# Plain 128-row blocks for x and the result, and a 128-row low-part pass of the scores, in a one-core transformer layer

## The chip, the cores and the metric

The kernel runs on one core of one Trainium2 chip. The metric is the device time of one execution in microseconds (us). Three runs of the kernel before gave 637.65, 639.62 and 641.45 us; the median is 639.62 us. One further execution was taken with the hardware profiler.

## The reference

One layer over 256 tokens of width 1024, in float32:

```python
cs = jax.nn.silu(c)
mod = cs @ ada_w[l] + ada_b[l]
sh1, sc1, g1, sh2, sc2, g2 = jnp.split(mod[:, None, :], 6, axis=-1)
h = rms_norm(x, norm1_g[l]) * (1.0 + sc1) + sh1
x = x + g1 * token_mixer(h, ...)
h = rms_norm(x, norm2_g[l]) * (1.0 + sc2) + sh2
x = x + g2 * hier_moe(h, ...)
return rms_norm(x, final_g)
```

`token_mixer` projects h with one wide matrix and runs two branches: a diagonal complex state-space scan with a gated output, and grouped attention (16 heads of 64, 4 key groups) with compressed, selected and window keys. `hier_moe` sends each token to 2 of 32 experts (1024 to 256 to 1024).

## The kernel before

**Order of tokens.** On the chip a block of 128 tokens does not lie in its natural order: row 32 j + c of block b holds token 128 b + 4 c + j, which is what the scan over chunks of four tokens wants. The order is made by the load of x (line 109): its source is a view "(c j) d -> j c d", four groups of 32 rows, each row 4 KB. The results leave through the inverse view (lines 1347 and 1355), as four transfers of 128 rows by 512 columns, 2 KB a row. Line 1355 issues each as soon as its part is scaled by line 1354 (VectorE) or lines 1351 and 1352 (ScalarE, then GpSimd).

**Start.** SyncE issues all plain loads in one in-order queue: x block 0, a small pack of constants (line 111), x block 1, then in turn the eight 1 MB slices of the modulation weights (`ada1`, line 121) and eight 512 KB slabs of the first projections (line 128), with further constants between. VectorE makes masks and index tiles (lines 143 to 185); GpSimd makes the identity, some iotas, and sets large tiles to zero: `Vc` (128 x 5120, line 489), `B0` (128 x 1024, line 491), `bw` (128 x 4096, line 493) and `Tt` (line 571). Per block of x, ScalarE sums squares (line 213), VectorE takes the reciprocal root (`rsqrt1`, lines 192 to 197) and scales (line 215), and TensorE transposes (line 219). Then a loop over eight slices (lines 357 to 374) makes the modulation vectors and the first four projections, while VectorE also prepares the scan.

**Three-pass matmuls.** Most products are done in float32r as three passes of a high and a low part (`mm3`, lines 270 to 273): high x high, high x low, low x high.

**Attention.** Each of the 16 heads has three score tiles s0, s1, s2, each made by `score` (line 881): a pass of 128 rows whose lower and upper 64 rows hold the high and the low part of q against the high part of the keys (`KS`, written twice, line 882), a pass of 64 rows for the high part of q against the low part of the keys (`KL`, line 883), then one or two bf16 matmuls that add masks (line 885). 48 score tiles in all. VectorE takes maxima (lines 891 to 893), ScalarE exponentials (line 900), GpSimd scales (line 905), TensorE transposes (lines 910 and 912) and multiplies by the values (line 922). Projections and gates are put between the heads as filler. `KL` has two key groups side by side on its upper and lower 64 rows.

**After attention.** Output projections (lines 970 to 1033), then line 1041 puts the residual x into four accumulators `acc` by a matmul with the identity, in the order in which x lies. The experts (lines 1274 to 1300) gather tokens with 0/1 matrices, stream 96 MB of weights through rings of buffers (lines 1284 to 1291), and add their results to `acc` with 0/1 matrices built from token numbers `tok1` (lines 182 to 185). Two sums of squares and `rsqrt1` end the kernel.

**What sets the order.** The framework lays out the instructions of each engine at build time, by the order of the program and a simulated time line of its own, and adds the waits. Each engine then runs its list in that order.

Of the kernel before, what the change touches and what calls it, by code (L numbers as in the profile page):

```python
# [9 lines left out]
F32 = mybir.dt.float32  # L10
F32R = mybir.dt.float32r
BF16 = mybir.dt.bfloat16
AF = mybir.ActivationFunctionType
ALU = mybir.AluOpType
# [39 lines left out]
def hybrid(ctx: ExitStack, tc: tile.TileContext, A, out, dbg=None, stop=None):  # L54
    nc = tc.nc
# [5 lines left out]
    def f32(ap):  # L61
        return ap.bitcast(F32)
# [44 lines left out]
    x = cp.tile([128, 2, D], F32, name="x")  # L107
    for b in range(2):
        nc.sync.dma_start(x[:, b], A["x"][0, 128 * b:128 * b + 128].rearrange("(c j) d -> j c d", j=4))
        if b == 0:  # L110
            nc.sync.dma_start(pk[:, 0:NPK0], A["pk"][:, 0:NPK0])
# [25 lines left out]

    ident = cp.tile([128, 128], F32, name="ident")
    G.memset(ident, 1.0)  # L140
# [40 lines left out]
    V.tensor_scalar(desc, itok1[:, 0:8], -1.0, 9.0, op0=ALU.mult, op1=ALU.add)  # L181
    iq1 = pp.tile([128, 2, 2], I32, name="iq1")
    G.iota(iq1, pattern=[[128, 2], [0, 2]], base=1, channel_multiplier=1)
    tok1 = cp.tile([128, 2, 2], F32, name="tok1")
    V.tensor_copy(tok1, iq1)

# [198 lines left out]
    Tt = sp.tile([128, 16, 128], F32, name="Tt")  # L385
    Vc = sp.tile([128, 16, 2, 160], F32, name="Vc")
    Vt = Vc[:, :, :, 32:160]
# [100 lines left out]

    G.memset(Vc, 0.0)
    B0 = pp.tile([128, 16, 2, 32], F32, name="B0")  # L490
    G.memset(B0, 0.0)
    bw = pp.tile([128, 16, 2, 128], F32, name="bw")
    G.memset(bw, 0.0)
    bcur = [[pp.tile([128, 16, 16], F32, name=f"b{r}{i}") for r in range(2)] for i in range(2)]
# [178 lines left out]
    KS = at.tile([128, 4, 528], F32R, name="KS")  # L673
    KL = at.tile([128, 2, 528], F32R, name="KL")

    def keys(nm, offs):
        o = proj_T(nm)
        for gp in range(2):
            own = slice(64 * gp, 64 * gp + 64)
            for b in range(2):  # L680
                src = o[own, :, 128 * b:128 * b + 128]
                for hv in range(2):
                    hs = slice(64 * hv, 64 * hv + 64)
                    dst = KS[hs].rearrange("p (m two) t -> p m two t", two=2)[:, :, gp, offs[b]:offs[b] + 128]
                    (S.copy if hv == gp else V.tensor_copy)(dst, src)
                V.tensor_sub(KL[own, :, offs[b]:offs[b] + 128], src,
                             f32(KS[own].rearrange("p (m two) t -> p m two t", two=2)[:, :, gp, offs[b]:offs[b] + 128]))
# [33 lines left out]
    for g in range(4):  # L721
        gs = slice(64 * (g % 2), 64 * (g % 2) + 64)
        S.copy(KS[:, g, 256:272], pkc[:, 16 * g:16 * g + 16])
        V.tensor_sub(KL[gs, g // 2, 256:272], pkc[gs, 16 * g:16 * g + 16], f32(KS[gs, g, 256:272]))
    vcn = at.tile([64, 64], F32, name="vcn")
# [130 lines left out]
    for qc in range(4):  # L856
# [13 lines left out]
        for ii in range(2):  # L870
            for gp in range(2):
# [3 lines left out]
                nm = f"{qc}{ii}{gp}"  # L875
                q_hi = QS[own, ii, gp]
                s0 = psb.tile([128, 512], F32, name=f"s0{nm}", tag="s", bufs=3)
# [3 lines left out]
                def score(s_, t0, c0, n, masks):  # L881
                    T.matmul(s_[:, 0:n], lhsT=QS[:, ii, gp, t0:t0 + 128], rhs=KS[:, g, c0:c0 + n], start=True, stop=False)
                    T.matmul(s_[:, 0:n], lhsT=q_hi[:, t0:t0 + 128], rhs=KL[own, G2_, c0:c0 + n], start=False, stop=False)  # L883
                    for z, (a_, b_, m_) in enumerate(masks):
                        T.matmul(s_[:, a_:b_], lhsT=identb, rhs=m_, start=False, stop=z == len(masks) - 1)
# [73 lines left out]
    mgs = ctx.enter_context(ExitStack())  # L959
    mg = mgs.enter_context(tc.tile_pool(name="mg", bufs=1))  # L960
    G2, sh2 = Gm[:, 1], modT[:, 2]
    g1b, g2b = gb
# [75 lines left out]
    with tc.issue_after(pe_last[0].ins):  # L1038
        for h in range(2):
            for b in range(2):  # L1040
                T.matmul(acc[b][h], lhsT=ident, rhs=x[:, b, 512 * h:512 * h + 512], start=True, stop=False)
    dbg("x2", x)
# [302 lines left out]
    for b in range(2):  # L1345
        rsqrt1(rstd3[:, b:b + 1], ss3[:, b, 1:2], part3[:, b:b + 1], mo, f"r3{b}")
    ov = out[0].rearrange("(b c j) d -> b j c d", b=2, j=4)
    for b, c0, n in ((0, 0, 512), (0, 512, 512), (1, 0, 512), (1, 512, 512)):
        c, a_ = slice(c0, c0 + n), acc[b][c0 // 512][:, c0 % 512:c0 % 512 + n]
        if (b, c0) == (1, 0):  # L1350
            S.activation(x[:, b, c], a_, AF.Copy, scale=rstd3[:, b:b + 1])  # L1351
            G.tensor_mul(x[:, b, c], x[:, b, c], fg[:, c])  # L1352
        else:
            V.scalar_tensor_tensor(x[:, b, c], a_, rstd3[:, b:b + 1], fg[:, c], op0=ALU.mult, op1=ALU.mult)  # L1354
        nc.sync.dma_start(ov[b][:, :, c], x[:, b, c])
    return

def _lay(i):
# [50 lines left out]
    o["adat"] = np.stack([a.transpose(1, 0, 2) for a in two + one])  # L1410
    for n in ("x", "ada_b"):
        o[n] = i[n]
    o["fg"] = i["final_g"][None]
# [21 lines left out]
```

## Time and profile before

| what | us |
|---|---|
| median of three runs | 639.62 |
| the profiled execution's own time | 639.31 |
| span of the profile, first to last instruction | 637.6 |
| busy in the span: TensorE matmul (PE) / weight load (PEld) | 521.3 / 357.3 |
| busy in the span: VectorE (DVE) / ScalarE (ACT) / GpSimd (POOL) | 358.9 / 205.3 / 219.2 |
| moved by DMA | 168.11 MB |

A busy share is a mean over stages with different limits; the rows further down are therefore taken stage by stage. A matmul's duration in the profile contains its way through the pipeline, so the pace of TensorE is read from the distance of the starts of two matmuls. "PEclk" is the granted TensorE clock (1.00 is 2.4 GHz, 0.50 is 1.2 GHz). "DMA share" is the mean busy share of the core's 16 DMA engines.

### The profile page before, as it was taken

The numbers are of one execution on the slowest core, as the hardware profiler recorded it, in microseconds if no ns is written. First come the engines' busy times: TensorE is split into PE (matmuls) and PEld (weight loads), VectorE is DVE, ScalarE is ACT, GpSimd is POOL, SyncE is SP. The second block draws the span as 40 slices with busy tenths as digits, with TensorE's granted clock in tenths as the row PEclk, the third lists the DMA queues.
The fourth block names the chain that finished last, engine by engine and source line by source line (L and its number), as shares of the span: only waits on it lengthen the run. The fifth ranks groups of instructions, "written<-read, shape, count | busy, mean of one in ns | idle before, by whom it ended". The sixth has DMA issues, their size and how long they took to land. (4 is left out here: it accounts for less than half of the span.)

```text
span 637.6 us, 10548 instructions
## 1 busy us (share of the span) xinstructions
PE 521.3 (82%) x4027; PEld 357.3 (56%) x4028; DVE 358.9 (56%) x940; ACT 205.3 (32%) x469; POOL 219.2 (34%) x316
## 2 busy tenths in 40 slices
PE   0367799688887999999999996999988887867760
PEld 0255588477886878788888994443442242312120
DVE  9699965999476766567776767433330222302041
ACT  1365336433244554354543453112120111101030
POOL 7058405567478432696987005000000000000000
PEclk9997899797998999999999999799997999979795
DMA  8885355766545332653379797199999999999941
GB/s 175 283 325 176 114 186 187 275 228 256 196 155 182 117 100 67 222 198 142 94 269 346 284 421 291 62 371 398 423 418 423 419 420 422 420 421 420 408 167 67
DMA packets 27795, 168.11 MB, mean 264 GB/s; under 512 B 3034, under 2 KB 3162, under 8 KB 10202
## 3 DMA queue, kind: packets, MB, share of 16 engines
q1 hardware_dynamic: 25434, 158.97, 65.5%
q0 software_dynamic: 2304, 8.39, 3.9%
q8 instruction: 34, 0.56, 0.4%
q14 instruction: 23, 0.19, 0.1%
HBM read 166.30 MB, written 1.05 MB: 262 GB/s over the span
## 5 line engine op out<-in xcount | busy, mean ns | idle before, releaser
L1191 PE MATMUL guq<-gu,x 128*32 128x512 f32 (+1 forms) x512 | 101.0, 673 | 27.0 <-DMA gu<-in_egu_dram 26.3
L1352 POOL TENSOR_TENSOR x<-x,fg 128x512 f32<-128x512 f32 x1 | 1.3, 1267 | 222.3 <-ACT x L1351 222.3
L1191 PEld LDWEIGHTS guq<-gu,x 128*32 128x32 f32 (+1 forms) x512 | 22.9, 124 | 85.5 <-DMA gu<-in_egu_dram 46.4
L905 POOL TENSOR_SCALAR pr<-pr,st 128x128 f32<-128x128 f32 (+1 forms) x64 | 35.9, 577 | 35.2 <-DVE st L902 29.2
L336 POOL TENSOR_SCALAR adt<-adt,ct 128x256 f32<-128x256 f32 x64 | 39.6, 633 | 22.5 <-DMA adt<-in_adat_dram 22.3
L1212 PE MATMUL dnq<-ed,acq 128*32 128x512 f32 (+1 forms) x224 | 39.0, 598 | 2.8 <-ACT acq L1206 1.9
L1200 DVE SCALAR_TENSOR_TENSOR pk<-pk,guq 128x256 f32<-128x256 f32 x9 | 3.8, 420 | 62.5 <-ACT pk L1199 62.5
L1216 DVE SCALAR_TENSOR_TENSOR gb<-dnq,wsq,gb 128x512 f32<-128x512 f32 (+1 forms) x20 | 13.8, 696 | 40.5 <-PE dnq L1212 40.5
L1162 DVE TENSOR_SCALAR x<-pgq,Gm,modT 128x256 f32<-128x256 f32 (+1 forms) x20 | 10.3, 516 | 43.4 <-PE pgq L1156 23.4
L900 ACT ACTIVATE pr<-s,st 128x128 f32<-128x128 f32 (+1 forms) x64 | 26.1, 420 | 24.0 <-DVE st L896 22.8
L1160 ACT ACTIVATE x<-pgq,modT,Gm 128x256 f32<-128x256 f32 (+1 forms) x20 | 10.8, 541 | 56.0 <-DVE x L1162 25.9
L1217 ACT CAST room<-gb 128x512 fp32r<-128x512 f32 (+1 forms) x20 | 11.4, 575 | 53.5 <-DVE gb L1216 53.5
L1156 PE MATMUL pgq<-room,hTh 128*128 128x256 f32 (+1 forms) x80 | 22.9, 316 | 3.1 <-DVE wsq L1179 1.2
L1199 ACT ACTIVATE pk<-guq 128x256 f32<-128x256 f32 x9 | 3.5, 385 | 66.6 <-PE guq L1191 66.6
L1156 PEld LDWEIGHTS pgq<-room,hTh 128*128 128x128 f32 x80 | 16.1, 202 | 15.6 <-issue 5.7
L1212 PEld LDWEIGHTS dnq<-ed,acq 128*32 128x32 f32 (+1 forms) x224 | 10.7, 113 | 23.4 <-issue 17.6
L219 PE MATMUL ph<-ident,scr 128*128 128x128 f32 x16 | 3.1, 358 | 24.7 <-DVE rstd L197 24.7
L337 POOL TENSOR_TENSOR adt<-adt 128x512 f32<-128x512 f32 x16 | 23.0, 1447 | 0.5
L230 PE MATMUL pm<-ada,csb 128*32 128x256 f32 x256 | 19.7, 415 | 3.8 <-DVE mr L240 3.8
L1156 PE MATMUL pgq<-room,hTl 128*128 128x256 f32 (+1 forms) x80 | 21.1, 294 | 0.0
L883 PE MATMUL s<-KL,QS 64*128 64x272 f32 (+1 forms) x48 | 18.7, 390 | 0.0
L1072 POOL TENSOR_SCALAR gb<-x,rstd 128x256 f32<-128x256 f32 x8 | 4.0, 515 | 39.4 <-ACT xT L1008 39.3
(718 smaller groups left out, 1729.9 us busy)
## 6 DMA issues: line engine op xcount, KB each, us to landing
gu<-in_egu_dram SPq DMA_DIRECT2D x64, 1024.0 KB, 19.8
ed<-in_edn_dram SPq DMA_DIRECT2D x28, 1024.0 KB, 18.0
ada<-in_adat_dram SPq DMA_DIRECT2D x16, 1024.0 KB, 8.8
adt<-in_adat_dram POOLq DMA_DIRECT2D x16, 512.0 KB, 6.1
slab<-in_w_dram SPq DMA_DIRECT2D x8, 512.0 KB, 3.8
cw<-in_cw_dram SPq DMA_DIRECT2D x4, 1024.0 KB, 4.9
win_q<-in_win_dram SPq DMA_DIRECT2D x4, 1024.0 KB, 4.9
win_gs<-in_win_dram SPq DMA_DIRECT2D x4, 1024.0 KB, 7.4
```

The costliest lines, as they stand in the source:

```text
L230: T.matmul(pm_k[32 * t:32 * t + 32, 0:256], lhsT=csb[:, 2 * t + j], rhs=slot[:, 2 * t + j], start=j == 0, stop=j == 1, tile_position=(0, 3 ...
L336: G.tensor_scalar(w[:, t], w[:, t], ct[:, 4 * h + t:4 * h + t + 1], 1.0, op0=ALU.mult, op1=ALU.mult)
L337: G.tensor_add(w[:, 0:2], w[:, 0:2], w[:, 2:4])
L883: T.matmul(s_[:, 0:n], lhsT=q_hi[:, t0:t0 + 128], rhs=KL[own, G2_, c0:c0 + n], start=False, stop=False)
L900: S.activation(pr[:, a_:b_], src, AF.Exp, bias=st[:, 1, z:z + 1], scale=0.125, accum_out=st[:, 2, z:z + 1])
L905: G.tensor_scalar(pr[:, a_:b_], pr[:, a_:b_], st[:, 3, z:z + 1], 1.0, op0=ALU.mult, op1=ALU.mult)
L1156: T.matmul(pg[:, ki, 0:S_], lhsT=h[:, b, 128 * k:128 * k + 128], rhs=O[:, b], start=b + i == 0, stop=b + i == 2)
L1160: S.activation(xk[:, ki, 0:S_], pg[:, ki, 0:S_], AF.Identity, bias=sh2[:, k:k + 1], scale=G2[:, k:k + 1])
L1191: gl_ = T.matmul(gu[r], lhsT=xe[k][:, r], rhs=wgu(e, k), start=k == 0, stop=k == 7, tile_position=(0, s_ * e))
L1212: T.matmul(dn[r], lhsT=ac[:, c, r], rhs=wdn(e, c)[:, 512 * h:512 * h + 512], start=c == 0, stop=c == 1, tile_position=(0, s_ * e))
L1216: V.scalar_tensor_tensor(ty[0:M, c], dn[0:M, c], ws[0:M, 0:1], g2b[0:M, 512 * h + c.start:512 * h + c.stop], op0=ALU.mult, op1=ALU.mult)
L1217: act_last[0] = S.copy(yh[0:M, h, c], ty[0:M, c])
```

## The change

- x is laid out on the host in the order in which the chip wants it; each block is loaded as plain 128 rows.
- A 0/1 matrix `perm` (one VectorE instruction) takes the place of the identity in the four matmuls that put x into `acc`, so that `acc` is in natural order; `tok1` gets permuted token numbers to match; the result leaves as plain 128 rows.
- `KL` becomes 128 rows for each of the four key groups, with zeros in the half that does not belong to the group (two new GpSimd memsets); the low-part pass takes the same 128-row weights as the pass before it.
- The zeroing of `Vc` and `bw` moves from GpSimd to VectorE and to the head of the program; an iota of GpSimd and a cast of VectorE become two small VectorE instructions.

```diff
-        nc.sync.dma_start(x[:, b], A["x"][0, 128 * b:128 * b + 128].rearrange("(c j) d -> j c d", j=4))
+        nc.sync.dma_start(x[:, b], A["x"][b])
...
+    Vc = sp.tile([128, 16, 2, 160], F32, name="Vc")
+    V.memset(Vc, 0.0)
+    bw = pp.tile([128, 16, 2, 128], F32, name="bw")
+    V.memset(bw, 0.0)
     ident = cp.tile([128, 128], F32, name="ident")
...
-    iq1 = pp.tile([128, 2, 2], I32, name="iq1")
-    G.iota(iq1, pattern=[[128, 2], [0, 2]], base=1, channel_multiplier=1)
     tok1 = cp.tile([128, 2, 2], F32, name="tok1")
-    V.tensor_copy(tok1, iq1)
+    for b in range(2):
+        V.tensor_scalar(tok1[:, b], tq.to_broadcast([128, 2]), 128.0 * b + 1.0, None, op0=ALU.add)
...
-    G.memset(Vc, 0.0)
...
-    G.memset(bw, 0.0)
...
-    KL = at.tile([128, 2, 528], F32R, name="KL")
+    KL = at.tile([128, 4, 528], F32R, name="KL")
+    for gp in range(2):
+        G.memset(f32(KL[64 - 64 * gp:128 - 64 * gp].rearrange("p (m two) t -> p m two t", two=2)[:, :, gp]), 0.0)
...
-        V.tensor_sub(KL[gs, g // 2, 256:272], pkc[gs, 16 * g:16 * g + 16], f32(KS[gs, g, 256:272]))
+        V.tensor_sub(KL[gs, g, 256:272], pkc[gs, 16 * g:16 * g + 16], f32(KS[gs, g, 256:272]))
...
                     T.matmul(s_[:, 0:n], lhsT=QS[:, ii, gp, t0:t0 + 128], rhs=KS[:, g, c0:c0 + n], start=True, stop=False)
-                    T.matmul(s_[:, 0:n], lhsT=q_hi[:, t0:t0 + 128], rhs=KL[own, G2_, c0:c0 + n], start=False, stop=False)
+                    T.matmul(s_[:, 0:n], lhsT=QS[:, ii, gp, t0:t0 + 128], rhs=KL[:, g, c0:c0 + n], start=False, stop=False)
...
+    perm = mg.tile([128, 128], F32, name="perm")
+    V.tensor_scalar(perm, itok1[:, 0:128], tq, 1.0, op0=ALU.subtract, op1=ALU.is_equal)
...
-                T.matmul(acc[b][h], lhsT=ident, rhs=x[:, b, 512 * h:512 * h + 512], start=True, stop=False)
+                T.matmul(acc[b][h], lhsT=perm, rhs=x[:, b, 512 * h:512 * h + 512], start=True, stop=False)
...
-    ov = out[0].rearrange("(b c j) d -> b j c d", b=2, j=4)
+    ov = out[0].rearrange("(b p) d -> b p d", b=2)
...
-        nc.sync.dma_start(ov[b][:, :, c], x[:, b, c])
+        nc.sync.dma_start(ov[b][:, c], x[:, b, c])
...
-    for n in ("x", "ada_b"):
-        o[n] = i[n]
+    o["x"] = i["x"][0].reshape(2, 32, 4, 1024).transpose(0, 2, 1, 3).reshape(2, 128, 1024)
+    o["ada_b"] = i["ada_b"]
```

## Rows read from the trace of the kernel before

**Rows 1.** Busy time of each engine in stretches of the span (from the span's start), with the number of instructions; then the granted TensorE clock, the DMA share and GB/s.
```profile
24.00:87.00 63.00, 47.34 (x388) 36.19 (x389) 59.12 (x219) 29.86 (x59) 29.82 (x38) 0.89 0.60 221
200.00:320.00 120.00, 119.52 (x903) 99.97 (x902) 82.19 (x195) 59.78 (x170) 74.37 (x116) 0.99 0.38 131
...
400.00:410.00 10.00, 9.26 (x36) 5.08 (x38) 2.71 (x20) 1.50 (x4) 0.00 (x0) 0.62 0.01 2
...
413.00:613.00 200.00, 167.94 (x970) 64.84 (x972) 46.51 (x112) 25.41 (x51) 0.00 (x0) 0.95 1.01 411
```

**Rows 2.** Waits: who waited for whom, us in total, times, longest. The first is the longest of VectorE from 24 to 87 us, the second the only one of TensorE's matmuls from 200 to 320 us.
```profile
DVE mr L240 <- PE pm L238: 1.2, 2, 1.0
...
PE pj_ga L273 <- DVE ga2l L264: 0.5, 1, 0.5
```

**Rows 3.** The time line from 0 to 30 us: start, duration, engine, line and operation; in brackets the engine's idle time before it and what ended it.
```profile
1.08 0.17 DVE L319 MEMSET onesc<- 128x128 f32 x1
...
1.40 0.22 DVE L149 CAST tk<-itok 128x128 f32<-128x128 int32 x1
1.41 0.06 DVE L1132 MEMSET own<- 64x2 f32 x1
...
2.09 0.59 SPq L109 DMA_DIRECT2D x<-in_x_dram  x1
...
2.14 4.35 POOL L489 MEMSET Vc<- 128x5120 f32 x1
2.21 10.55 DVE L143 CAST identb<-ident 128x128 bf16<-128x128 f32 x1
...
10.88 1.79 POOL L571 MEMSET Tt<- 128x2048 f32 x1
...
21.84 1.06 ACT L213 ACTIVATE scr<-x 128x1024 f32<-128x1024 f32 x1 [5.68 <-DMA x<-in_x_dram]
...
23.02 0.15 DVE L192 TENSOR_SCALAR r11v<-ss 128x1 f32<-128x1 f32 x1 [5.94 <-ACT scr L213]
...
24.69 1.94 PE L219 MATMUL ph<-ident,scr 128*128 128x128 f32 x8 [24.69 <-DVE rstd L197]
```

**Rows 4.** Two stretches of 1 us at the start, columns as in Rows 1: while the second block of x is on its way, and just after it has landed.
```profile
18.00:19.00 1.00, 0.00 (x0) 0.00 (x0) 0.00 (x0) 0.00 (x0) 0.00 (x0) 1.00 1.01 217
...
22.00:23.00 1.00, 0.00 (x0) 0.00 (x0) 0.00 (x0) 0.99 (x2) 0.00 (x0) 1.00 1.01 406
```

**Rows 5.** The two passes of the scores by their lines: min/median/max ns of one, first and last start, shapes.
```profile
L882 PE MATMUL s<-KS,QS x48: 275/288/428, 180.7 to 320.1; 128*128 128x272 f32 x32, 128*128 128x256 f32 x16
...
L883 PE MATMUL s<-KL,QS x48: 379/387/490, 181.0 to 320.4; 64*128 64x272 f32 x32, 64*128 64x256 f32 x16
```

**Rows 6.** The time line of TensorE (columns as in Rows 3) at two score tiles: around 209 us, and at a bf16 mask matmul behind a float32 transposition at 249 us.
```profile
209.21 0.28 PE L271 MATMUL pj_q<-hTh,q1h 128*128 128x256 f32 x1
209.21 0.19 PEld L882 LDWEIGHTS s<-KS,QS 128*128 128x128 f32 x1
...
209.33 0.28 PE L882 MATMUL s<-KS,QS 128*128 128x272 f32 x1
209.54 0.18 PEld L883 LDWEIGHTS s<-KL,QS 64*128 64x128 f32 x1
209.54 0.39 PE L883 MATMUL s<-KL,QS 64*128 64x272 f32 x1
...
209.87 0.29 PE L885 MATMUL s<-mask,identb 128*128 128x272 bf16 x1
...
249.80 0.33 PE L910 MATMUL pta<-ident,pr 128*128 128x128 f32 x1
...
249.97 0.22 PE L885 MATMUL s<-mask,identb 128*128 128x128 bf16 x1
```

**Rows 7.** The time line (columns as in Rows 3) of GpSimd's scaling and of the transpositions that follow it, in two heads.
```profile
239.32 1.62 POOL L905 TENSOR_SCALAR pr<-pr,st 128x128 f32<-128x128 f32 x4 [4.81 <-DVE st L902]
...
243.66 0.24 PEld L910 LDWEIGHTS pta<-ident,pr 128*128 128x128 f32 x2
...
270.90 0.48 POOL L905 TENSOR_SCALAR pr<-pr,st 128x256 f32<-128x256 f32 x1
...
271.47 0.24 PEld L910 LDWEIGHTS pta<-ident,pr 128*128 128x128 f32 x2
```

**Rows 8.** TensorE just after a wait: the time line at 200 us, and a stretch of 2 us with PE's busy time, the clock, the DMA share and GB/s.
```profile
200.70 0.41 PE L273 MATMUL p<-yTh,wso0l 128*128 128x256 f32 x1
...
200.91 0.41 PE L271 MATMUL p<-yTh,wso0h 128*128 128x256 f32 x1
...
200.00:202.00 2.00, 2.00 (x12) 0.50 0.21 86
```

**Rows 9.** The end: the time line (columns as in Rows 3), then stretches of 1 us (columns as in Rows 1): one of the last loads, one while the result leaves, and the last one with data.
```profile
621.47 2.07 DVE L1354 SCALAR_TENSOR_TENSOR x<-acc,rstd,fg 128x512 f32<-128x512 f32 x3 [0.66 <-PEq L1320]
...
622.30 3.89 SPq L1355 DMA_DIRECT2D out_dram<-x  x4
...
609.00:610.00 1.00, 0.53 (x7) 0.21 (x7) 0.00 (x0) 0.38 (x1) 0.00 (x0) 1.00 1.06 391
...
629.00:630.00 1.00, 0.00 (x0) 0.00 (x0) 0.00 (x0) 0.00 (x0) 0.00 (x0) 0.50 0.27 106
...
635.00:636.00 1.00, 0.00 (x0) 0.00 (x0) 0.00 (x0) 0.00 (x0) 0.00 (x0) 0.50 0.15 57
```

More of the change, by code (lines that the diff above doesn't have):

```diff
@@ L385, in hybrid @@
     Tt = sp.tile([128, 16, 128], F32, name="Tt")
-    Vc = sp.tile([128, 16, 2, 160], F32, name="Vc")
     Vt = Vc[:, :, :, 32:160]
@@ L487, in h3 @@
         return a.rearrange("p (g h) -> p g h", g=16)
-    G.memset(Vc, 0.0)
     B0 = pp.tile([128, 16, 2, 32], F32, name="B0")
     G.memset(B0, 0.0)
-    bw = pp.tile([128, 16, 2, 128], F32, name="bw")
-    G.memset(bw, 0.0)
     bcur = [[pp.tile([128, 16, 16], F32, name=f"b{r}{i}") for r in range(2)] for i in range(2)]
@@ L685, in keys @@
                     (S.copy if hv == gp else V.tensor_copy)(dst, src)
-                V.tensor_sub(KL[own, :, offs[b]:offs[b] + 128], src,
+                V.tensor_sub(KL[own].rearrange("p (m two) t -> p m two t", two=2)[:, :, gp, offs[b]:offs[b] + 128], src,
                              f32(KS[own].rearrange("p (m two) t -> p m two t", two=2)[:, :, gp, offs[b]:offs[b] + 128]))
@@ L875, in hybrid @@
                 nm = f"{qc}{ii}{gp}"
-                q_hi = QS[own, ii, gp]
                 s0 = psb.tile([128, 512], F32, name=f"s0{nm}", tag="s", bufs=3)
```

## The prediction

> **What bounds the kernel now.** I read the stage windows first, then waits, then the time lines of the places that the diff touches. No single engine bounds the whole. From 24 to 87 us VectorE is busy 59.1 of 63 us and its longest wait is 1.2 us in total [rows 1, 2]: VectorE bounds. From 200 to 320 us TensorE is busy 119.5 of 120 us and its only wait is 0.5 us [rows 1, 2]: TensorE bounds. From 413 to 613 us all DMA engines are busy at 411 GB/s while TensorE is at 168 of 200 us: the expert weights bound. Before that, from 400 to 410 us, DMA stands still (share 0.01) because every buffer is full [rows 1]. So a stage that ends earlier lets the next start earlier: the weight stream of the last third is tied to buffers that the stages before give back, and those 10 us of full buffers are slack in it. I count gains ahead of 413 us one for one.
>
> Two stretches have no bound of that kind, and the change touches both. At the start TensorE does nothing until 24.69 us, released by VectorE's reciprocal root of the second block of x; VectorE had idled 5.94 us for ScalarE's squares of that block, and those started at 21.84 us, when the block landed, 19.7 us after its issue at 2.09 [rows 3]. Before that, VectorE sat 10.55 us in one small cast (its like took 0.22 us) from 2.21 to 12.76 us, just while GpSimd's memsets ran, the last from 10.88 to 12.67 us [rows 3]. At the end, the results are computed by 623.54 us (621.47 + 2.07), but data still move at 106 GB/s with a DMA share of 0.27 until within the stretch that begins at 635 [rows 9]. A share of about a quarter is four of 16 engines, and the transfers of line 1355 have an outer loop of four, as those of x have.
>
> **Part 1: the start.** VectorE loses 10.55 - 0.22 = 10.3 us in the cast and 5.9 us in the wait, 16.3 us together. The change removes the long memsets from GpSimd; the two that stay ahead of the loop run while VectorE is at its own memsets. It loads x over all engines. Two blocks are 1.05 MB: at 217 GB/s, the rate while they were on their way, 4.8 us; at 406 GB/s, the rate right after [rows 4], 2.6 us; issued by 2.7 us, and with an estimated 2 us to the first data and 1 to be noticed, the second block is there at 8 to 10.5 us in place of 21.8. What it adds: VectorE sets 9,216 columns to zero. 128 columns took 0.17 us and 2 took 0.06 [rows 3], so 0.87 ns a column: 8.0 us, from about 1 to 9 us, and behind it in VectorE's list wait the identity's cast, all masks and the chain to the transpositions. They have no other way round: the memsets are on VectorE's path now, hidden only by the landing of x, and now about as long. The two `tok1` instructions against the cast: 0.2 us. VectorE bounds up to 87 us, so the gain is its lost time less its new work: 16.3 - 8.0 - 0.2 = 8 us. Ends: 10 if the memsets go faster than their short likes (GpSimd's ran at 4.35 us for 5,120 columns), 3 if a wait for a weight slice opens behind the earlier start.
>
> The Trainium skill ("VectorE: DVE Perf Modes", Zero memsets can be issued as uint32) says that a memset takes one cycle per element, which at its 0.96 GHz would be 9.6 us for 9,216; by that estimate part 1 would give 6.5 and the total below 614.5. The short memsets of the trace read faster; a long one on VectorE is in no row of before.
>
> **Part 2: the low-part pass.** In a stream of 128-row passes a start follows the last by 0.12 us (209.21 to 209.33), with the next weights loading meanwhile. At the 64-row pass its weights start only with the matmul itself, 0.21 us after the 128-row pass, and the bf16 mask starts 0.33 us after it [rows 6]. The pass lasts 387 ns against 288 for its 128-row neighbour, in all 48 tiles [rows 5]. With 128 rows I expect 0.12 into the pass, a gain of 0.09. Out of it, part of the 0.33 may belong to the step from float32 to bf16: a mask behind a transposition started 0.17 us after it [rows 6], so I take 0.17, a gain of 0.16. 48 x 0.25 = 12 us. Ends: 48 x 0.09 = 4.3 us if the way out costs the same as now; 48 x 0.30 = 14.4 if 0.12 holds on both sides. Less what waits take back: a head gets 0.75 us faster on TensorE, while maxima, exponentials and scaling do not. In one head GpSimd is done at 240.94 us and the last transpositions load at 243.66 or later, 2.7 us of room; in another it is done at 271.38 and they load at 271.47, no room [rows 7]. If four of 16 heads are tight, some 2 us return as waits. I take 10.
>
> **Part 3: the result.** 1.05 MB at 106 GB/s are 10 us; over 16 engines at the 391 GB/s of the last loads [rows 9] 2.7 us. Four issues take 3.9 us from 622.30 now; nothing else is in that queue, and the last part is ready at 623.5 whatever the layout. With the last issue at about 624.5 and an estimated 2 us from issue to data, the last byte goes at 627 in place of 635.6: 8.5 us. Ends: 6 if writes over 16 engines reach half the rate of loads, 9.5 if they keep up with the issue.
>
> **Edits at nothing.** The two zeroings of `KL` (1,056 columns each, by GpSimd's 0.85 ns some 0.9 us) fall where GpSimd waits for the scan; if that cover goes, 1.8 us. `perm` is one VectorE instruction of 128 columns, about 0.2 us (as the cast), in a stage that TensorE bounds. The matmuls with `perm` have the identity's shape. The host's order of x costs the chip nothing.
>
> **Sum.** 8 + 10 + 8.5 = 26.5 us off the profiled execution's 639.31 (span 637.6; 0.3 under the median of the runs, 639.62): **613 us**. About 0.5% (3 us) is what a measurement of this kernel can tell from no change.
>
> **Rivals.**
> 1. *The low-part pass gives little*: the way out of it costs as before, or the head's chain over VectorE, ScalarE and GpSimd takes TensorE's place. For: the tight head [rows 7]. Against: 0.5 us of waits in 120 us [rows 2]. Part 2 falls to 4, or near 0: 619 to 623 us. The Trainium skill ("TensorE: Matmul & The Clock Gate", Why this matters for your kernels) says that a single K=32 matmul takes the same time as one of K=128, by which fewer rows are no loss to undo; the rows contradict this here, where the 64-row pass holds up both neighbours.
> 2. *The start does not move through*: the new order of VectorE's list, or slices that land late, spend part 1 before 87 us. For: VectorE's and GpSimd's work there is interleaved by a simulation that does not know the 10.55 us. Against: the busy 59 of 63 us. Part 1 is 0 to 3: 618 to 621 us.
> 3. *The result is not limited by its four engines* but by the memory's side: part 3 falls to 2, 619 us. Against: a share of 0.27 at 629 us [rows 9].
> 4. *Slower, by TensorE's clock.* Just after TensorE's wait near 198 us the granted clock was 0.50 (1.2 GHz) and starts came 0.21 us apart in place of 0.12 [rows 8]. If a TensorE that is faster than the head's chain waits in every head, and the clock falls after each wait, a matmul costs 0.09 us more: 903 of them from 200 to 320 us are 81 us. The point at which it outweighs the gain: 26.5 / 0.09 = 295 matmuls at the low clock, a third of the stage. At half the stage, 639 + 41 - 26 = 654 us. Against: the clock stood at 0.99 there [rows 1].
> 5. *More than forecast*: every part at its upper end, 639.3 - 34 = 605.
>
> **Chances.** Forecast, within about 6 us of 613: 0.57. Rival 1: 0.15. Rival 2: 0.12. Rival 3: 0.04. Rival 5: 0.07. Rival 4: 0.03, and 0.02 that gains and losses cancel. The range takes in the forecast, one failing part, and the upper ends: 604 to 624. Faster 0.95, within 0.5% 0.02, slower 0.03.
>
> **What would show it.** Part 1: TensorE's first transposition near 16.5 us, no cast above 0.3 us, two VectorE memsets of 4 to 5 us at the head, and the end of the VectorE-bound stage 8 us earlier. Part 2: starts 0.12 apart into line 883, at most 0.17 out of it, durations of that line near 288 ns, and the stretch from the first score tile to the last about 10 us shorter. Part 3: a DMA share near 1 at the end, and some 5 us from the last VectorE instruction to the end of the span in place of 14. The prediction is wrong if the first transposition is early but the expert stage starts no earlier, if the stretch of the scores keeps its length, or if the last transfers still take 10 us.

## The result, and the profile after

The changed kernel takes 614.72 us (median of four runs, 610.37 to 617.20) against 639.33 us for four runs of the kernel before beside it: a ratio of 0.961, 95% interval 0.954 to 0.967. Its profiled execution took 615.27 us, with a span of 613.5 in place of 637.6. The forecast was 613. Further down, one run of the low-part pass alone (636.88 us) lies over 1.5% above the fastest of its kernel and is left out of that kernel's median and ratio.

Where the 24.0 us of span went is read from the starts of instructions that exist in both kernels. The table gives them in us from the span's start; the last five columns are kernels of the next section.

| start of | before | after | x alone | memsets alone | KL alone | result alone | memsets split |
|---|---|---|---|---|---|---|---|
| first transposition of x | 24.69 | 20.58 | 18.49 | 33.65 | 23.21 | 24.51 | 15.66 |
| first score pass | 180.67 | 172.40 | 174.43 | 183.84 | 180.93 | 182.23 | 163.47 |
| last score pass | 320.36 | 302.33 | 313.78 | 323.44 | 311.00 | 320.61 | 291.08 |
| first expert matmul | 402.15 | 386.00 | 396.28 | 405.58 | 394.55 | 401.59 | 375.00 |
| first final scaling (VectorE) | 621.47 | 606.61 | 615.71 | 625.07 | 614.46 | 620.13 | 593.73 |
| end of the span | 637.58 | 613.54 | 631.79 | 641.18 | 630.53 | 627.11 | 600.84 |

Column "after" less column "before": 8.3 us gained at the first score, 9.8 more over the scores, 1.9 given back between the last score and the experts, 1.3 in the experts' stage, and 9.2 gained behind the last scaling: 8.3 + 9.8 - 1.9 - 1.3 + 9.2 = 24.1.

The stage windows of after, with the columns of [rows 1]: the start's rest, the scores, the stretch in which every buffer is full, and the experts.

```profile
24.00:79.00 55.00, 43.34 (x336) 33.32 (x336) 53.31 (x198) 26.26 (x51) 31.50 (x38) 0.88 0.57 206
200.00:302.00 102.00, 99.67 (x840) 88.89 (x838) 77.74 (x182) 55.42 (x159) 66.08 (x104) 1.00 0.41 141
388.00:390.00 2.00, 2.00 (x10) 1.77 (x12) 0.00 (x0) 0.00 (x0) 0.00 (x0) 0.50 0.00 0
397.00:597.00 200.00, 168.73 (x965) 65.06 (x966) 46.31 (x111) 25.45 (x51) 0.00 (x0) 0.94 1.01 411
```

VectorE still bounds the first stage (97% busy). TensorE does 840 matmuls in 102 us of the scores at a clock of 1.00, but is now idle for 2.3 us there, against 0.5 of 120 us in [rows 1]. DMA still stands still before the experts and then runs at 411 GB/s, as before.

The start, to be set against [rows 3] (time line: start, duration, engine, line and operation; in brackets the idle time before it and what ended it):

```profile
1.98 4.33 DVE L140 MEMSET Vc<- 128x5120 f32 x1 [1.86 <-issue]
4.49 1.06 ACT L216 ACTIVATE scr<-x 128x1024 f32<-128x1024 f32 x1 [2.37 <-DMA x<-in_x_dram]
7.11 3.47 DVE L142 MEMSET bw<- 128x4096 f32 x1 [0.80 <-issue]
7.68 1.06 ACT L216 ACTIVATE scr<-x 128x1024 f32<-128x1024 f32 x1 [1.95 <-DMA x<-in_x_dram]
11.22 0.21 DVE L147 CAST identb<-ident 128x128 bf16<-128x128 f32 x1
11.79 0.14 DVE L195 TENSOR_SCALAR r11v<-ss 128x1 f32<-128x1 f32 x1
12.53 1.23 DVE L369 TENSOR_TENSOR sl<-slab,sh 128x1024 fp32r<-128x1024 f32 x1 [0.53 <-ACT sh L368]
16.65 1.93 PE L233 MATMUL pm<-ada,csb 128*32 128x256 f32 x16 [16.65 <-DVE csb L209]
20.58 0.69 PE L222 MATMUL ph<-ident,scr 128*128 128x128 f32 x2 [0.75 <-DVE scr L218]
```

The second block of x is there at 7.7 us, not at 21.8. The cast takes 0.21 us, not 10.55. But VectorE's two memsets run from 1.98 to 10.55 us, and the reciprocal root of block 1, whose sum of squares is ready at 8.8, starts at 11.79. TensorE's first work is now the modulation (line 233), not the transpositions.

The score passes, by lines as in [rows 5], and the time line of one of them as in [rows 6]:

```profile
L882 PE MATMUL s<-KS,QS x48: 279/290/428, 172.4 to 302.1; 128*128 128x272 f32 x32, 128*128 128x256 f32 x16
...
L883 PE MATMUL s<-KL,QS x48: 276/287/428, 172.6 to 302.3; 128*128 128x272 f32 x32, 128*128 128x256 f32 x16
```
```profile
200.20 0.28 PE L882 MATMUL s<-KS,QS 128*128 128x272 f32 x1
200.20 0.19 PEld L883 LDWEIGHTS s<-KL,QS 128*128 128x128 f32 x1
200.32 0.29 PE L883 MATMUL s<-KL,QS 128*128 128x272 f32 x1
200.44 0.10 PEld L885 LDWEIGHTS <-identb 128*128 128x128 bf16 x1
200.45 0.29 PE L885 MATMUL s<-mask,identb 128*128 128x272 bf16 x1
```

Both passes last the same, and the starts are 0.12 and 0.13 us apart, with the weights of the low-part pass loading under the pass before it.

The end, as [rows 9], with windows of 1 us behind the last scaling:

```profile
606.61 2.07 DVE L1356 SCALAR_TENSOR_TENSOR x<-acc,rstd,fg 128x512 f32<-128x512 f32 x3
...
607.45 2.45 SPq L1357 DMA_DIRECT2D out_dram<-x  x4
```
```profile
609.00:610.00 1.00, 0.00 (x0) 0.00 (x0) 0.00 (x0) 0.00 (x0) 0.00 (x0) 0.50 0.79 285
610.00:611.00 1.00, 0.00 (x0) 0.00 (x0) 0.00 (x0) 0.00 (x0) 0.00 (x0) 0.50 1.01 381
611.00:612.00 1.00, 0.00 (x0) 0.00 (x0) 0.00 (x0) 0.00 (x0) 0.00 (x0) 0.50 0.36 135
```

The DMA share reaches 1.01; the data are out in the stretch that begins at 611, 2.3 to 3.3 us behind VectorE's end (606.61 + 2.07), where it took 11.5 to 12.5 before.

### The profile page after: what moved, and what is told of

The parts are those of the page before. It is cut to its first block, busy times and chain, and to the rows that moved or that the text cites. A ratio compares the mean times of both kernels' runs of the same rounds, so it can differ in the third digit from the quotient of the medians.

```text
span 613.5 us, 10554 instructions
## 1 busy us (share of the span) xinstructions
PE 512.7 (84%) x4027; PEld 354.2 (58%) x4028; DVE 360.3 (59%) x944; ACT 205.1 (33%) x469; POOL 214.7 (35%) x315
## 5 line engine op out<-in xcount | busy, mean ns | idle before, releaser
L1193 PE MATMUL guq<-gu,x 128*32 128x512 f32 (+1 forms) x512 | 102.7, 685 | 27.2 <-DMA gu<-in_egu_dram 26.4
L905 POOL TENSOR_SCALAR pr<-pr,st 128x128 f32<-128x128 f32 (+1 forms) x64 | 36.2, 582 | 29.0 <-DVE st L902 21.8
L233 PE MATMUL pm<-ada,csb 128*32 128x256 f32 x256 | 21.2, 421 | 21.3 <-DVE csb L209 16.6
L1164 DVE TENSOR_SCALAR x<-pgq,Gm,modT 128x256 f32<-128x256 f32 (+1 forms) x20 | 10.3, 516 | 42.3 <-PE pgq L1158 25.0
L1158 PEld LDWEIGHTS pgq<-room,hTh 128*128 128x128 f32 x80 | 16.1, 201 | 16.0 <-issue 5.7
L233 PEld LDWEIGHTS pm<-ada,csb 128*32 128x32 f32 x256 | 7.4, 115 | 28.7 <-DVE csb L209 16.3
L1214 PEld LDWEIGHTS dnq<-ed,acq 128*32 128x32 f32 (+1 forms) x224 | 11.1, 113 | 20.7 <-issue 16.5
L340 POOL TENSOR_TENSOR adt<-adt 128x512 f32<-128x512 f32 x16 | 21.6, 1358 | 0.5
L910 PE MATMUL pta<-ident,pr 128*128 128x128 f32 x64 | 14.8, 282 | 2.5 <-POOL pr L905 2.3
```

What stands on the lines that cost most here:

```text
L233: T.matmul(pm_k[32 * t:32 * t + 32, 0:256], lhsT=csb[:, 2 * t + j], rhs=slot[:, 2 * t + j], start=j == 0, stop=j == 1, tile_position=(0, 3 ...
L340: G.tensor_add(w[:, 0:2], w[:, 0:2], w[:, 2:4])
L905: G.tensor_scalar(pr[:, a_:b_], pr[:, a_:b_], st[:, 3, z:z + 1], 1.0, op0=ALU.mult, op1=ALU.mult)
L910: T.transpose(dst, pr[:, c0:c0 + 128], ident)
L1158: T.matmul(pg[:, ki, 0:S_], lhsT=h[:, b, 128 * k:128 * k + 128], rhs=O[:, b], start=b + i == 0, stop=b + i == 2)
L1193: gl_ = T.matmul(gu[r], lhsT=xe[k][:, r], rhs=wgu(e, k), start=k == 0, stop=k == 7, tile_position=(0, s_ * e))
```

## The experiments

### One part at a time

Each of these is the kernel before with one part of the change.

```diff
 # x alone
-        nc.sync.dma_start(x[:, b], A["x"][0, 128 * b:128 * b + 128].rearrange("(c j) d -> j c d", j=4))
+        nc.sync.dma_start(x[:, b], A["x"][b])
 # memsets alone: at the head
+    V.memset(Vc, 0.0)
+    V.memset(bw, 0.0)
...
-    G.memset(Vc, 0.0)
-    G.memset(bw, 0.0)
 # KL alone (tile, zeroing and writes of KL as in the change)
...
-                    T.matmul(s_[:, 0:n], lhsT=q_hi[:, t0:t0 + 128], rhs=KL[own, G2_, c0:c0 + n], start=False, stop=False)
+                    T.matmul(s_[:, 0:n], lhsT=QS[:, ii, gp, t0:t0 + 128], rhs=KL[:, g, c0:c0 + n], start=False, stop=False)
 # result alone: perm, tok1 (as in the change) and the store
...
-        nc.sync.dma_start(ov[b][:, :, c], x[:, b, c])
+        nc.sync.dma_start(ov[b][:, c], x[:, b, c])
```

**x alone.** 

> The kernel before with x laid out on the host and loaded as plain 128-row blocks, nothing else. Theory A (the start has two losses that overlap: x lands late, and the cast beside GpSimd's memsets holds VectorE until 12.8 us): x lands before 9 us, VectorE's wait of 5.9 us goes, the cast stays at 10.5 us, no memset is added to VectorE; 5 to 6 us faster than before, about 634. Rival B (the late x is the whole loss of the start): 8 us or more, 631 or less. Rival C (the cast alone sets the start): within 1 us of before.

Measured: 630.41 us, ratio 0.987 (0.984 to 0.990). In its trace:

```profile
2.21 10.55 DVE L143 CAST identb<-ident 128x128 bf16<-128x128 f32 x1
...
8.18 1.06 ACT L213 ACTIVATE scr<-x 128x1024 f32<-128x1024 f32 x1 [2.24 <-DMA x<-in_x_dram]
...
10.89 1.79 POOL L571 MEMSET Tt<- 128x2048 f32 x1
...
18.49 0.87 PE L219 MATMUL ph<-ident,scr 128*128 128x128 f32 x3 [18.49 <-DVE r__641 L412]
```

The cast keeps its 10.55 us, ended by the end of GpSimd's last memset, and TensorE still starts 6.2 us earlier; 5.8 us of it arrive at the end of the span. By the trace that is theory A. But the traced execution, at 633.52 us, was the slowest of the five; by the medians the gain is 8.5 us, with an interval of 6.6 to 10.4, nearer to B. So it is shown that the cast stays and that x moves the start; how much of the start's loss x alone was is not settled.

**Memsets alone.** 

> The kernel before with the zeroing of Vc and bw moved to VectorE and to the head, nothing else; x is still loaded in four groups of 32 rows. Theory A: the cast falls from 10.5 to 0.2 us, but VectorE has 8 to 9 us of its own memsets and still waits for x block 1 at 21.8 us: 0 to 2 us faster, 638 to 639.5. Rival B (the contention of GpSimd's memsets with VectorE is the start's loss): 6 us or more, 633 or less. Rival C (memsets on VectorE cost more than the stall that they remove): 2 us or more slower.

Measured: 642.67 us, ratio 1.005 (1.003 to 1.008): slower, as rival C has it. But not for its reason:

```profile
20.93 1.06 ACT L217 ACTIVATE scr<-x 128x1024 f32<-128x1024 f32 x1 [8.42 <-DMA x<-in_x_dram]
...
25.48 1.23 DVE L370 TENSOR_TENSOR sl<-slab,sh 128x1024 fp32r<-128x1024 f32 x1 [3.15 <-ACT sh L369]
...
29.79 1.94 PE L234 MATMUL pm<-ada,csb 128*32 128x256 f32 x16 [29.79 <-DVE csb L210]
```

VectorE's memsets end at 10.55 us, far ahead of x. But the new list has the first steps on x's second block, for which VectorE waits 9.28 us, and then the split of the first weight slab (line 370) ahead of the masks, `csb` and the rest of the chain of x. That slab lands behind the slow x, VectorE waits 3.15 us for it, and TensorE starts at 29.79. In the changed kernel the same order costs a wait of 0.53 us (line 369), because everything lands earlier.

**KL alone.** 

> The kernel before with KL of 128 rows for each of the four groups, nothing else. Theory A (the pass's two changes of row count cost 0.09 us in and 0.19 us out, 48 times, and what is not given back as waits in the heads stays): the score stretch from first to last pass is 9 to 11 us shorter, then the last head's scaling waits on GpSimd and takes 1.5 to 2 back, so the expert stage starts about 8 us earlier: about 631. Rival B (the 2 us were lost by the earlier start, not by the pass): 10 us, 629. Rival C (the pass's gain needs the other parts): 4 us or less.

Measured: 628.68 us (three runs), ratio 0.984 (0.981 to 0.988), which is 7.6 to 12.4 us and cannot tell A from B. From first to last score pass 130.07 us against 139.69; from there to the first expert matmul 83.55 against 81.79. Theory A holds in both numbers of the trace: 9.6 gained, 1.8 given back, and this without an earlier start, against rival B.

**Result alone.** 

> The kernel before with perm in the four residual matmuls, tok1 to match and the result written as plain 128 rows, nothing else. Theory A (four of 16 engines carry the result in four groups): nothing changes up to the last VectorE instruction, then 4.5 to 5.5 us to the end of the span in place of 14.0, DMA share near 1 there: 9 us faster, 630 to 631. Rival B (the memory side limits the write): 2 us or less.

Measured: 630.31 us, ratio 0.989 (0.986 to 0.992). From the first final scaling to the end 7.0 us against 16.1: 9.1 us, as in the changed kernel (6.9). Theory A.

By the ratios x, KL and the result alone make 1.3 + 1.6 + 1.1 = 4.0%; the whole change makes 3.9%. Within the intervals the parts add up, and the moved memsets have no share that can be seen.

### The memsets

These four are the changed kernel with the zeroing placed differently.

```diff
 # back on GpSimd at the old place
-    V.memset(Vc, 0.0)
-    V.memset(bw, 0.0)
...
+    G.memset(Vc, 0.0)
...
+    G.memset(bw, 0.0)
 # split
-    V.memset(bw, 0.0)
+    G.memset(bw, 0.0)
 # mirror of the split
-    V.memset(Vc, 0.0)
+    G.memset(Vc, 0.0)
 # all on VectorE, at the head
+    V.memset(B0, 0.0)
...
+    V.memset(Tt, 0.0)
...
-    G.memset(B0, 0.0)
...
-    G.memset(Tt, 0.0)
```

**Back on GpSimd.** 

> The changed kernel with the zeroing of Vc and bw back on GpSimd at its old place; x, KL and the result as changed. Theory A (x alone brings its 6 us, and the memsets' move adds 2 on top because VectorE's list behind it is another): first score near 174.5 us in place of 172.4, 617 us. Rival B (the memsets' move is worth nothing once x lands early): 614 to 615. Rival C (it is the larger half of the start): 620 or more.

Measured: 616.47 us, ratio to the kernel before 0.963 (0.960 to 0.966), against 0.961 (0.954 to 0.967) for the change: no difference. The first score is at 172.00 us, with the move at 172.40. Rival B. (With x alone, whose start is the same, it was 174.43. So two kernels can differ by some 2 us at this place for reasons that lie between.)

**Split.** 

> The changed kernel with the zeroing of bw on GpSimd at the head, that of Vc on VectorE as changed. Theory A (VectorE's two memsets, 8.6 us from start to end, hold the root of x's second block by 2.7 us, since its squares are read at 8.8 and the root starts at 11.7): VectorE is free at 7.1 us, root near 9 to 9.5, first transposition near 18, 2 to 2.5 us faster than the changed kernel, 612. Rival B (GpSimd's memset stalls VectorE's casts again as before, until it ends near 8 us): 1 us or less gained. Rival C (the order of VectorE's list, not the memsets, sets the start): no gain or a loss.

Measured: 603.48 us, ratio 0.944 (0.939 to 0.948), far below any of the three forecasts.

```profile
0.83 3.51 POOL L142 MEMSET bw<- 128x4096 f32 x1 [0.29 <-POOLq L1427]
1.98 4.33 DVE L140 MEMSET Vc<- 128x5120 f32 x1 [1.86 <-issue]
...
5.98 1.79 POOL L570 MEMSET Tt<- 128x2048 f32 x1
...
6.59 1.22 DVE L405 TENSOR_SCALAR r__643<-pk 128x16 f32<-128x16 f32 x1
6.78 1.06 ACT L216 ACTIVATE scr<-x 128x1024 f32<-128x1024 f32 x1 [1.03 <-DMA x<-in_x_dram]
...
7.97 0.14 DVE L195 TENSOR_SCALAR r11v<-ss 128x1 f32<-128x1 f32 x1
...
10.57 1.94 PE L233 MATMUL pm<-ada,csb 128*32 128x256 f32 x16 [10.57 <-DVE csb L209]
...
15.66 0.69 PE L222 MATMUL ph<-ident,scr 128*128 128x128 f32 x2 [1.81 <-DVE scr L218]
```

Rival B's stall is there (line 405 needs 1.22 us and ends with GpSimd's memset), but the root of block 1 starts at 7.97, right behind its squares, in place of 11.79. TensorE starts 6.1 us earlier, the transpositions 4.9. The first score is 8.9 us earlier and the end 12.7. VectorE was spared 3.47 + 0.80 = 4.3 us. By the table, the split is ahead of the change by 4.9 us at the transpositions, 8.9 at the first score, 11.3 at the last, 11.0 at the first expert matmul and 12.9 at the final scaling. So what is gained beyond the 4.3 is spread over the stages up to there. The build did find another order: TensorE's list differs from the projections of the first slice on (25.35 us in the changed kernel). In the scores two waits of TensorE, 1.8 us for ScalarE (line 831) and 1.1 for VectorE's split of `wso0` (line 267), are not there. That the order brought the rest is not shown by an experiment.

**Mirror.** 

> The mirror of the split: Vc (5,120 columns) is zeroed by GpSimd at the head, bw (4,096) by VectorE. Theory A (what counts is when VectorE and GpSimd are both done with the long memsets): VectorE free at 5.5 us, but its first operation on data stalls until GpSimd's last memset ends near 8.7, so TensorE's first work within 1 us of the split kernel's 10.6, and the time within 4 us of its 603.5. Rival B (the split kernel's further 4 to 6 us came from a lucky order of the lists after the start): 609 or more.

Measured: 608.71 us, ratio 0.952 (0.947 to 0.958). TensorE's first work at 10.69 us, the first score at 168.33. The start is as theory A has it; the time lies between A's bound and B's, and its interval overlaps the change's. So in this trace splitting the memsets brings some 4 us at the first score (172.40 to 168.33). The split's further 5 do not come from an earlier start: the mirror's first transposition, at 14.22 us, is ahead of the split's, at 15.66. The order that the build finds is what is left to explain them; it is not shown.

**All on VectorE.** 

> The changed kernel with all four long memsets (B0 and Tt too, 3,072 columns more) on VectorE at the head. Theory A (VectorE's memsets lie on the path of the start): by 0.85 ns a column 2.6 us later at TensorE's first work (16.65 in the changed kernel), and 2 to 4 us slower, 617 to 619. Rival B (GpSimd's two remaining memsets hold VectorE or anything else): no loss or a gain. Rival C (the lists' order decides, not the memsets): a change of the time without that shift at the start.

Measured: 616.73 us, ratio 0.962 (0.957 to 0.968). TensorE's first work is at 20.50, 3.9 us later; the first score at 176.58, 4.2 later; the first expert matmul at 389.50, 3.5 later; the end only 1.4. Theory A for the start; the time cannot be told from that of the change.

### What the 64-row pass cost

```diff
-                    T.matmul(s_[:, 0:n], lhsT=QS[:, ii, gp, t0:t0 + 128], rhs=KS[:, g, c0:c0 + n], start=True, stop=False)
-                    T.matmul(s_[:, 0:n], lhsT=QS[:, ii, gp, t0:t0 + 128], rhs=KL[:, g, c0:c0 + n], start=False, stop=False)
+                    T.matmul(s_[:, 0:n], lhsT=QS[own, ii, gp, t0:t0 + 128], rhs=KS[own, g, c0:c0 + n], start=True, stop=False)
+                    T.matmul(s_[:, 0:n], lhsT=QS[own, ii, gp, t0:t0 + 128], rhs=KL[own, g, c0:c0 + n], start=False, stop=False)
```

> The changed kernel with both passes of a score on the same 64 rows (own half of QS against own half of KS, then of KL): the products of q's low part are left out. Theory A (each change of the number of rows costs, not the 64 rows themselves): 0.12 to 0.13 us from the first pass to the second, 0.32 out of the second to the mask, 0.21 or more into the first; the stage 6 to 9 us longer than the changed kernel. Rival B (each 64-row pass costs by itself): 0.2 to 0.3 us also between the two 64-row passes, the stage 12 us or more longer.

Measured: 621.15 us (two runs), ratio 0.969 (0.965 to 0.974). By the time line:

```profile
201.35 0.28 PE L274 MATMUL pj_q<-hTh,q1h 128*128 128x256 f32 x1
201.56 0.39 PE L882 MATMUL s<-KS,QS 64*128 64x272 f32 x1
201.79 0.28 PE L883 MATMUL s<-KL,QS 64*128 64x272 f32 x1
202.01 0.29 PE L885 MATMUL s<-mask,identb 128*128 128x272 bf16 x1
```
```profile
201.56 0.18 PEld L882 LDWEIGHTS s<-KS,QS 64*128 64x128 f32 x1
201.67 0.19 PEld L883 LDWEIGHTS s<-KL,QS 64*128 64x128 f32 x1
202.00 0.10 PEld L885 LDWEIGHTS <-identb 128*128 128x128 bf16 x1
```

The starts are 0.21, 0.23 and 0.22 us apart, as neither theory had put it; read with the weight loads they say what costs. The first 64-row pass starts 0.09 late, its weights start only with it, and it lasts 0.39. The second one's weights load under the first, 0.11 behind it, and it lasts 0.28 like a pass of 128 rows. Then the mask starts 0.09 late. I read this as 0.09 to change over, 0.1 for weights that could not be loaded ahead and 0.09 to change back: 0.28 us in all, for one 64-row pass before [rows 6] and for two here. In sum, the second of the two costs nothing extra. The stage is 139.4 us long again, as in the kernel before (139.7).

### The wait that took the last head's place

Time line of after, GpSimd and TensorE, at the last head (its factors are ready from VectorE at 307.79 us):

```profile
305.98 1.28 POOL L340 TENSOR_TENSOR adt<-adt 128x512 f32<-128x512 f32 x1
309.67 2.33 POOL L339 TENSOR_SCALAR adt<-adt,ct 128x256 f32<-128x256 f32 x4 [2.41 <-DMA adt<-in_adat_dram]
...
312.40 0.33 PE L910 MATMUL pta<-ident,pr 128*128 128x128 f32 x1 [1.73 <-POOL pr L905]
```

GpSimd waits for a slice of the last modulations (its list has them ahead of the scaling of line 905), and TensorE for GpSimd. I took the last head's scaling off GpSimd:

```diff
-                    G.tensor_scalar(pr[:, a_:b_], ...)
+                    (V if (qc, ii, gp) == (3, 1, 1) else G).tensor_scalar(pr[:, a_:b_], ...)
```

> The changed kernel with the scaling of the last head's scores on VectorE in place of GpSimd. Theory A (that scaling is ready at 307.8 us and sits until 312.0 on GpSimd behind a product that waits for its own transfer; TensorE idles 1.7 us): the idle goes, the last head ends 1.5 us earlier, 613. Rival B (TensorE had to wait for another thing at that place): no change in the last head's end. Rival C (VectorE's extra work there delays the splits of weights that follow): a loss of 0.5 us or more.

Measured: 612.09 us, ratio 0.956 (0.953 to 0.959), not to be told from the change's. That TensorE wait is gone, but the stretch from the last score pass to the first expert matmul is 83.57 us against 83.67: TensorE waits 1.1 us for a split of the output projection's weights on VectorE (line 267) and 0.3 for its ScalarE half. Rival C in kind; what this execution had gained, it had gained ahead of the last score. Nor does the stretch need that edit to be shorter: it is 82.3 us with the zeroing back on GpSimd and in the mirror and 82.7 with all of it on VectorE, where the last head is as in the change but waits 0.7, 0.3 and 0 us for GpSimd. The last head's scaling was also moved together with the split of the memsets:

> The split (bw on GpSimd at the head) and the last head's scaling on VectorE together. Theory A (the last head waits 2.3 us for GpSimd in the split kernel, and only for that): that wait goes, about 601.5. Rival B (the DMA-bound stage behind takes it back): 603.5 as the split alone.

Measured: 608.68 us, ratio 0.949 (0.944 to 0.954), 5 us behind the split alone and so worse than either theory. The longest wait of TensorE from 300 to 372 us, and what held VectorE and GpSimd before it:

```profile
PE p L276 <- DVE nwo1l L267: 4.8, 1, 4.8
```
```profile
317.29 3.79 DVE L982 TENSOR_TENSOR t_ga<-t_ga,t_gs 128x512 f32<-128x512 f32 x1
321.00 1.74 DVE L267 TENSOR_TENSOR nwo1l<-nwo,nwo1h 128x1024 fp32r<-128x1024 f32 x1
...
316.67 2.49 POOL L340 TENSOR_TENSOR adt<-adt 128x512 f32<-128x512 f32 x2
```

VectorE is late here for the most part not by the scaling that it took over. One addition (line 982), ahead of the split that TensorE waits for, lasts 3.79 us while GpSimd multiplies and adds its modulations beside it; the median of that line is 0.69. The split lasts 1.74 us in place of 1.2. That is 3.6 of the 4.8 us. The stretch behind the last score is 87.1 us. The second such kernel moves one more head's scaling:

> As the kernel before it, and the scaling of the last head of the third group on VectorE too, where the split kernel's TensorE idles 1.3 us for GpSimd. Theory A (each of these waits is passed on): 1 us less again, about 600.5. Rival B (VectorE, which splits the next weights, is then late for them): 601.5 or more.

Measured: 607.94 us, ratio 0.949 (0.944 to 0.954). By the time that is rival B, but its weights are not late. The stretch behind the last score is 81.2 us, less than in the kernel before (81.8), and it is the scores that are longer: 134.0 us against 127.6 in the split alone. There VectorE's line 896, four columns with a median of 0.22 us, lasts 5.22 us, from 282.28 until the last of a row of GpSimd's instructions on the modulations ends at 287.47. TensorE then waits 3.1 us for the exponentials that follow it, and its granted clock is 0.91 from 280 to 300 us. So in both kernels the time went where VectorE's work on data ran beside GpSimd's. I read this from one trace each; no experiment keeps the two apart. The fastest version of the study is the split alone, 603.48 us.

## Why the prediction was right, and where it was not

**The total** was forecast at 26.5 us off and came to 24.6 (medians), 24.0 by the spans. The likeliest case happened, and each part has its sign and nearly its size; in part 1 the size is in part luck, as the next paragraph shows.

**Part 1, forecast 8, was 8.3 at the first score, with its shares wrong.** The sum held 5.9 for x and 10.3 - 8.0 - 0.2 = 2.1 for the memsets. x alone gave 6.2. The memsets' term failed: alone they cost 3.2, on top of x they brought between -0.4 and 2.0 (by the kernel with the zeroing back on GpSimd and by that with x alone), and no median shows it. The price per column was right (4.33 us for 5,120 is 0.85 ns; forecast 0.87). The step that failed is "from about 1 to 9 us", with the list behind the memsets taken as it was: they began at 1.98, stood 0.80 between the two, and ended at 10.55, so VectorE had no room left ahead of x. And the list behind them was not the old one shifted: the slab's split and `csb` came ahead of the transpositions, which started at 20.58 and not near 16.5. The end of the VectorE-bound stage moved by 11 us (the first matmul of the scan, line 550, which follows it: 93.13 to 81.69) and not by 8; 3 of these were lost again by 172 us, in an order of the work that I did not take apart.

The estimate from the Trainium skill ("VectorE: DVE Perf Modes", Zero memsets can be issued as uint32), 9.6 us for the 9,216 columns, lies above the two rows (4.33 + 3.47 = 7.8 us), and also above their whole stretch of 8.6. The measurement decides; that its total is near the measured one says nothing of the memsets, whose move has no share that can be seen.

**Part 2, forecast 10, was 9.8 over the scores and 7.9 at the experts.** Two steps of it were off. The way out of the pass: I had given part of the 0.33 us to the change from float32 to bf16 and kept 0.17; it is 0.13 now, so no cost of the change of type shows. By the medians, 0.219 to 0.127 into the pass and 0.319 to 0.129 out of it, the pace gains 48 x 0.28 = 13.5 us, not 12. What is taken back is 3.7 within the scores and 1.9 behind them, in place of 2. Of the 3.7, 2.4 show as idle time of TensorE between the first and the last pass (5.3 us before, 7.7 after), the rest I cannot place. The 2 us were the failing term: I looked for tight heads in the middle, and half of what came on top is at the last head, where the scaling queues behind GpSimd's modulations. It is no fixed price of the change, since three of the kernels with the zeroing elsewhere give back only 0.5 to 0.9.

What the 64-row pass cost is a change of the number of rows, as the two traces and the 64-row pair show. The Trainium skill ("TensorEngine Tiling (Array Packing)", Key Properties) says of the tiling modes of TensorE: "Mode switching requires drain". Whether a plain pass of 64 rows is such a switch it does not say there; the traces fit it, with 0.09 us on each side and 0.1 for the weights. The Trainium skill's other page, "TensorE: Matmul & The Clock Gate", from which I took the rival that fewer rows lose no time, is not contradicted by the rows, though I had said so: a 64-row pass behind its like lasts 0.28 us, as one of 128 does. It says nothing on the change between them, and that was the price.

**Part 3, forecast 8.5, was 9.2.** A share of 0.79 to 1.01 at 285 to 381 GB/s, 4.9 us from the last VectorE instruction to the end of the span (forecast 5). The issues also became cheaper, 2.45 us for four against 3.89. The sum had the rate of loads, 391 GB/s; the writes come near it.

**One for one** held within 1.3 us: from the first expert matmul to the first final scaling it is 219.3 us before, 220.6 after, and 218.5 to 220.6 in all kernels of the study.

**Rivals.** The clock (rival 4) stayed at 1.00 from 200 to 302 us. Rival 2's reason, the new order of VectorE's list, is what made the memsets alone 3.2 us slower, in the one kernel with them in which x stays slow. Rivals 1 and 3 did not happen.

## What to carry to other kernels

A pass with another number of rows between full ones is paid at both its borders, so look at the starts of the neighbours and at when its weights load, not at its duration. Work that "only" fills a buffer can go where both engines are idle: here the move of all of it from one engine to the other gave nothing that could be seen, and zeroing on both at once gave 11 us by the medians in one arrangement and 6, within the intervals, in the other; how much of that is the order of the lists is open. And a wait removed on one engine's list is worth what the next list leaves of it: measure at the next stage's first instruction, not at the wait, and compare an instruction that comes late with others of its own line.

## What the runs showed of the hardware that was not expected

- VectorE's memset is not slowed by a memset of GpSimd at the same time: `Vc` took 4.33 us beside GpSimd's `bw` (0.83 to 4.34 us) and 4.33 with GpSimd idle from 1.95 us on (all on VectorE). VectorE's first operation on data is slowed: line 405, 16 columns, took 1.22 us beside GpSimd's `Tt` and ended at 7.81, when that ended (7.77). The Trainium skill ("SBUF — State Buffer", Who interferes with whom) states that the two engines share a pair of ports, and that where both need it the first holds it for its whole instruction while the other stands. The traces agree that VectorE stands, but not that it is for one instruction: the cast of [rows 3] stood for 10.55 us, over several memsets of GpSimd of which the longest took 4.35.
- VectorE stands so in the middle of the kernel too: 5.22 us for four columns (line 896) and 3.79 for an addition of 0.69 (line 982), both beside GpSimd's work on the modulations.
- Between two long memsets VectorE stood for 0.80 us with nothing to wait for that the profile shows; with all four on VectorE it was 0.80, 0.16 and 0.38.
- The split and the kernel with the last head changed too have the same order up to the first score on VectorE, ScalarE and GpSimd, and up to 144 us on TensorE; their traced executions differ by 0.8 us at the first transposition (15.66 and 16.42) and by 2.5 at the first score (163.47 and 165.93). A stage's gain of 2 us or less is not to be read from one trace, and that holds for those of this text too.
